# Query and key of the first head pair ahead, x's second half behind two weight tiles, one product for the gates' partial sums, and mLSTM heads that wait for their own value alone

## The chip, the cores and the metric

The kernel runs on one core of a Trainium2 chip. A core has a matrix engine (PE, with its weight loads shown as PEld), a vector engine (DVE), a scalar engine (ACT), GpSimd (POOL) and a sync engine (SP) that here only issues DMAs. They run side by side, each through its own queue in order, and wait for one another by semaphores. The metric is device time in microseconds (us) of one execution; lower is better.

## The reference

It is one inference step of a two-layer decoder trunk. It works on 512 prompt tokens and on 32 sample tokens (8 sequences of 4) that bring recurrent states along. Layer 0 has a combined mixer: one input projection feeds four mLSTM heads and four GLA heads, and one output projection joins them. Layer 1 has a Mamba-2 mixer. Each mixer and each squared-ReLU MLP is followed by a residual sum and a layer norm. Outputs are the tokens and all new states, in float32. What matters here is the first mixer:

```python
mq, mk, mv, mo, mi, mf, gq, gk, gv, gg, ga = split(x @ w_in)
ig, lf = mi + ig_bias, log_sigmoid(mf + fg_bias)          # mLSTM gates, per token and head
ml_out = headnorm(mlstm(mq, mk, mv, ig, lf)) * sigmoid(mo)
la = log_sigmoid(ga @ wa2 + ba) / 16                      # GLA decay, per token and key feature
gla_out = headnorm(gla(gq, gk, gv, la)) * silu(gg)
mix = concat(ml_out, gla_out) @ w_out
```

## The kernel before

Activations lie feature-major: 128 features on the partitions, 544 tokens (512 and 32) along the rows, in two halves of 272. A float32 product is made of three fp32r products, high by high, high by low and low by high, so weights and activations are each split into a high part (a cast on ACT) and the rest (a subtraction on DVE). One weight tile is 1024 by 128; `dense` (L365) works through one tile and one half with 24 matmuls (L378) that sum in PSUM, and an evacuation takes the sum out.

`WeightStream` loads tiles in planned order over SP into three raw buffers and splits them (L167, L168) ahead of use; five split tiles are held. `take_x` loads x in pieces of two feature blocks. In it the order on SP, ACT and DVE is the written one: tile 0 with x's first half piece by piece, tile 1, then tiles 2 to 4 (`ws.ahead(HEAD)`), then x's second half (L295 on SP) with its splits (L287, L288). Constants, the selector, `wa2` and small states are loaded behind it (`issue_after(x_in)`).

In `ab` the input projection has 24 tiles: gq, gq, gk, gk, four gv, two mq, two mk, four mv, four gg, four mo (two heads share a q or k tile, a v or gate tile is one head's). The first `HEAD` = 5 tiles run on the first half one after another and then on the second; the next run both halves each, and the last four run as a group again. `evac` copies a projection out; gate tiles (gg, mo) take five operations on ACT and one or two on DVE for each half, all others a plain copy.

PE's order is written out by hand. Everything that isn't projection sits in **lanes**, generators that yield a number of ticks. `tick` is called ahead of each projection matmul and lets every lane count down by one, or run on to its next yield. So small products are laced between projection products at places set by the table `W` and by `need(key)`, which polls once a tick. The lanes are:

- `gla_lane`: waits for the gates, makes the decays (`la`, L1032, then a chain over ACT and DVE to `A`), and then scores for two head pairs q: query times key of the diagonal (`gd`, L1068), then nine levels of a halving scheme, each with a POOL subtraction F (L1079), two exponentials on ACT, `zq` and `zk` on DVE, and products `gs` (L1096, L1109), `W["lev"]` ticks apart. Then come the four heads (`head_out`: `num` L865, a norm over DVE and ACT to `hn`, its transpose `hot` L899), the final state, and the samples of GLA and mLSTM.
- `ml_lane`: `ml_gates`, then one pipeline of four heads (`ml_head`: `rowbc` L769; exponentials E on ACT; the masked key `kz` L1310; `md` and `mo` L1314 to L1321; then `head_out`), `W["mr"]` ticks between steps. In a full step PE issues `hot` of one head, `md` and `mo` of the next but one, `num` of the one between, and `rowbc` of the last. It starts when GLA is ready, mq and mk are there, and `mvt` says that all four values are in token order.
- the value lane: `tokmajor` transposes each value W["v"] = 24 ticks after its tile.

The gate projection (4 + 4 + 16 columns) doesn't go through `dense`: `gate_sums` multiplies eight narrow weight blocks in four column groups at a time, so a half's partial sums lie in four groups of 32 partitions; `gate_rows` (L849) joins them with three products of 4, 4 and 16 columns, and three ACT operations (L851) add the bias. `until("mheads")` in the last group of tiles runs the mLSTM lane to its end if it hasn't got there.

Of the kernel before, what the change touches and what calls it, by code (L numbers as in the profile page):

```python
# [31 lines left out]
HEAD, TAIL = 5, 7  # L32
HEADM = 6

W = dict(dec=12, gates=30, gr=8, sc=16, lev=14, v=24, kd=10, out=38, ss=40, end=12, c0=20, u=13, s=16, ml=12, mr=40, dt=238, sg=72, sx=14, sq=26, so=48, l0=12, l1=12, v0=74, v1=55, f0=16, f1=18, f2=4, ls=20, vs=47)
GATES = ((0, 0, 4), (32, 4, 4), (64, 8, 16))
# [20 lines left out]
def _consts():  # L57
    c = {}
    i = np.arange(P)
    c["ident"] = np.eye(P)  # L60
    for L in LEVELS:
        s, t = i[:, None], i[None, :]
        m = (s // (2 * L) == t // (2 * L)) & (s % (2 * L) < L) & (t % (2 * L) >= L)
        c[f"lv{L}"] = m[:, i % (2 * L) >= L]
    c["hm"] = np.stack([i < 64, i >= 64], 1)
    hs = np.zeros((P, 2, P))
    for h in range(4):
        hs[h, h // 2, (h % 2) * 64:(h % 2) * 64 + 64] = 1
    c["hfeat"] = hs
    hq = np.zeros((P, P)); hq[i // 32, i] = 1  # L70
    c["hstk"] = hq
    i4 = np.zeros((P, 4)); i4[:4] = np.eye(4)
    c["i4"] = i4
    c["hmask"] = i[:, None] // 32 == np.arange(4)[None]
    s, t = (i % 32)[:, None], np.arange(32)[None]
    c["smask"] = (s // LS == t // LS) & (s <= t)
    c["seye"] = s == t
    c["sl2"] = (s // 4 == t // 4) & (s % 4 < 2) & (t % 4 >= 2)
    c["sl1"] = (s // 2 == t // 2) & (s % 2 < 1) & (t % 2 >= 1)
    c["seqm"] = (i % 32)[:, None] // LS == np.arange(NB)[None]  # L80
    r = np.ones(T); r[NP::LS] = 0
    c["rmask"] = np.broadcast_to(r, (P, T))
    sel = np.zeros((P, 4, P))
    for h in range(4):
        sel[h, h] = 1
        sel[32 + h, h] = 1
    off, cols = {}, []
    n = 0
    for k, v in c.items():
# [139 lines left out]
def trunk_kernel(ctx, tc, a, stages=("ab", "mlp0", "ssd", "mlp1")):  # L229
# [61 lines left out]
    def take_x(pool, bufs=12, first=None):  # L291
# [8 lines left out]
        with tc.high_priority(), tc.manual_schedule(engines=order):  # L300
            ts = [load(S, 0, k)[0] for k in range(0, KT, 2)]
            S.preload_act_table_set("natural_log_exp_and_others")

            def step(k):
                cut(0, 2 * k, ts[k])
                if k == 1 and first is not None:
                    first()
            ws._emit([lambda k=k: step(k) for k in range(KT // 2)])
            ws._emit([lambda: None] * 4)
            ws.ahead(HEAD)  # L310
            for k in range(0, KT, 2):
                t, loaded = load(nc.sync, 1, k)
                ts.append(t)
                cut(1, k, t)
        with tc.issue_after(loaded):
            nc.sync.dma_start(out=lnp, in_=a["lnp"])
# [399 lines left out]
    def ab(pool, early, then):  # L716
# [19 lines left out]
        S.copy(selr, selt)  # L736
        prm = pool.tile([P, 13], F32, name="prm", bufs=1)
        G.dma_start(out=prm, in_=a["ab_prm"])
# [36 lines left out]
        gate = ft("gate")  # L775
        G.memset(gate[64:96], 0.0)
        fm = {}
# [3 lines left out]
        def tokmajor(key, h):  # L781
# [8 lines left out]
            for b in range(4):  # L790
                TE.transpose(p[:, b * P:(b + 1) * P], x[:, b * P:(b + 1) * P], ident)
            S.copy(vt[key][:, :, h, :128], p.rearrange("p (b c) -> p b c", b=4))
            G.tensor_copy(vraw[key][:, h], x[:, NP:])
            if h == 3:
# [9 lines left out]
        def evac(m, hf, ps):  # L804
# [20 lines left out]
            if hf == 1:  # L825
                ready.add(key)

        order = [(k, i) for k, n in (("gq", 2), ("gk", 2), ("gv", 4), ("mq", 2), ("mk", 2),
                                                     ("mv", 4), ("gg", 4), ("mo", 4)) for i in range(n)]

# [13 lines left out]
        def gate_rows(hf):  # L844

            c0, c1 = HALVES[hf]
            p = pm("gates")
            for o, c, n in GATES:
                TE.matmul(p[o:o + n, :TH], C("seye")[:, c:c + n], gsum[hf], start=True, stop=True)  # L849
            for o, c, n in GATES:  # L850
                S.activation(gate[o:o + n, c0:c1], p[o:o + n, :TH], AF.Identity, bias=gbias[o:o + n])  # L851
            if hf == 1:
                ready.add(("gate", 0))

        def head_out(mx, key, h, sT, enm=None):


            pp = [pm("num"), pm("num")]
            w = 128 if enm is None else 130
# [164 lines left out]
        def gla_decay():  # L1024
            gla["A"] = []
            for q in range(2):
                A = ft("A")
                t = ft("lat")
                for hf in range(2):
                    c0, c1 = HALVES[hf]  # L1030
                    p = pm("la")
                    TE.matmul(p[:, :TH], wa2[64:96, q * P:(q + 1) * P], gate[64:96, c0:c1], start=True, stop=True)  # L1032
                    S.activation(t[:, c0:c1], p[:, :TH], AF.Abs, bias=ba[:, q:q + 1])
# [8 lines left out]
        def gla_scores():  # L1042
# [4 lines left out]
            gla["kst"] = []  # L1047
            A, Q, K = gla["A"], [fm["gq", i] for i in range(2)], [fm["gk", i] for i in range(2)]
            zk = []
            for j in range(2):  # L1050
# [6 lines left out]
            n = 0  # L1057
            for q in range(2):
                sT = gla["sT"][q] = early.tile([P, 10, 2, P], F32, tag="sT", name="sT", bufs=2)

# [85 lines left out]
        def gla_sample_scores():  # L1146
# [3 lines left out]
            for L, mk in ((0, "seye"), (1, "sl1"), (2, "sl2")):  # L1150
# [24 lines left out]
                if L:  # L1175
                    V.copy_predicated(sst, C(mk).bitcast(U32), p[:, :NS])
                else:
                    V.tensor_tensor(sst, p[:, :NS], C(mk), ALU.mult)
            ready.add("sscores")
# [187 lines left out]
        def gla_lane():  # L1367
# [3 lines left out]
            yield from gla_decay()  # L1371
            yield from need(("gq", 1), ("gk", 1))
            yield from gla_scores()
# [8 lines left out]
            yield from gla_samples()  # L1382
            yield from need("mscores")
            yield from ml_samples()

        def ml_lane():
            ml["cg"] = []
            yield from need(("gate", 0))
            yield from ml_gates()
            yield from need("gla", ("mq", 1), ("mk", 1), "mvt")  # L1390
            rows_bc(ml["nM"][:, :NP])
# [17 lines left out]
        lanes.setdefault("ss", [])  # L1409
        heads = [ws.next() for _ in range(HEAD)]  # L1410
        for hf in range(2):
            for _ in gate_sums(1) if hf else ():
                pass
            for m, w in enumerate(heads):
                if hf and 1 <= m <= 2:
                    gate_rows(m - 1)
                dense(w, xrhs, KT, hf, lambda h, p, m=m: evac(m, h, p), first=(hf, m) == (0, 0))
        for m, key in enumerate(order[:-4]):
            if m >= HEAD:
                w = ws.next()  # L1420
# [594 lines left out]
def layout(i):  # L2015
# [15 lines left out]
    o["ab_gate"] = _blocks(g, 32)[0]  # L2031
    o["ab_in"] = _blocks(np.concatenate([seg(n) for n in ("gq", "gk", "gv", "mq", "mk", "mv", "gg", "mo")], 1), P)
    o["ab_out"] = _blocks(i["ab_w_out"][0], P)
    prm = np.zeros((P, 13), w.dtype)
    prm[0:4, 0], prm[32:36, 0] = i["ab_ig_bias"][0], i["ab_fg_bias"][0]
# [78 lines left out]
```

## Time and profile before

| what | us |
|---|---|
| median of three runs | 1495.31 (1493.13 to 1497.03) |
| profiled execution | 1494.75 |
| its span, first to last instruction | 1493.0 |
| input projection with its lanes (24 tiles, 1152 products) | ends at 246.7 |

The rest of the span is the output projection, two MLPs and the Mamba-2 mixer. In views of the trace a row gives the start in us, the us that it took, the engine, the line of the kernel, the operation, what it wrote and read, shapes and count; in brackets stands how long the engine had been idle and what ended it. Ends of matmuls are modelled, and one that is still draining counts as busy, so a wait can be longer for PE than its bracket says; the distance from start to start shows it. A float32 product with a full-precision operand has two records.

### The profile page before, as it was taken

The page shows a single profiled execution, that of the slowest core. Times are in us where ns is not written, and L with a number is a line of the kernel's source. Part 1 is how long each engine was busy: PE and PEld are TensorE (multiplying, and loading weights), DVE is VectorE, ACT ScalarE, POOL GpSimd, SP SyncE. Part 2 cuts the span into 40 slices and gives each one's busy share as a digit, 9 for nine tenths or more (in the row PEclk, how much of TensorE's full clock was granted, in tenths as well). Part 3 has the DMA queues.
Part 4 walks back from the last instruction along what each step waited for, and adds up shares of the span by engine and source line. Part 5 has one row for each costly group of instructions (what it writes and reads, how often), then busy time and mean ns, then how long its engine had stood idle before and what let it go on. Part 6 is the DMA issues. An engine that isn't in the chain of part 4 may idle for free.

```text
span 1493.0 us, 29232 instructions
## 1 busy us (share of the span) xinstructions
PE 1468.9 (98%) x11615; PEld 1417.0 (95%) x11615; DVE 1096.6 (73%) x2075; ACT 795.1 (53%) x1754; POOL 191.5 (13%) x225
## 2 busy tenths in 40 slices
PE   9999999999999999999999999999999999999997
PEld 8899989999999999999888789899999999999996
DVE  4966577786676667678999978777588677676656
ACT  6645556483543544547786676555257354444333
POOL 1510222100000000010244341421010000000000
PEclk9999999999999999999999999999999999999998
DMA  7221315313333332525567766364222333233121
GB/s 239 84 73 44 103 58 167 90 55 99 96 102 92 93 91 80 156 72 183 131 176 232 248 183 217 100 214 143 72 75 71 96 100 99 86 100 98 58 86 60
DMA packets 95025, 172.51 MB, mean 116 GB/s; under 512 B 15896, under 2 KB 50968, under 8 KB 94632
## 3 DMA queue, kind: packets, MB, share of 16 engines
q1 hardware_dynamic: 62280, 140.46, 30.7%
q10 hardware_dynamic: 29216, 17.19, 4.5%
q0 software_dynamic: 3392, 12.99, 2.4%
q8 instruction: 91, 1.49, 0.4%
q14 instruction: 46, 0.38, 0.1%
HBM read 153.48 MB, written 17.13 MB: 114 GB/s over the span
## 4 chain that ended last, share of the span: by engine, by line
PE 42%; DVE 4%; DMA 2%; issue 1%; ACT 1%; POOL 0%; SPq 0%; DVEq 0%; POOLq 0%; ACTq 0%
PE psd L378 29%; PE psd L590 9%; DVE wlo L168 1%; PE yp L1694 1%; DMA ec<-d_ecs 1%; DVE acc L1588 1%; PE it L1741 1%; DMA E<-d_cs 1%; PE sp L1672 1%; DMA wraw<-mlp_w 0%; PE sps L1748 0%; DVE h0n L1754 0%; PE ip L1669 0%; ACT E L1654 0%; PE xt L1633 0%
## 5 line engine op out<-in xcount | busy, mean ns | idle before, releaser
L378 PE MATMUL psd<-xh,whi 128*128 128x272 f32 x1488 | 441.5, 297 | 0.0
L378 PE MATMUL psd<-xh,wlo 128*128 128x272 f32 x1488 | 435.3, 293 | 0.0
L378 PE MATMUL psd<-xl,whi 128*128 128x272 f32 x1488 | 432.8, 291 | 1.3 <-DVE xl L478 1.3
L378 PEld LDWEIGHTS psd<-xh,whi 128*128 128x128 f32 x1488 | 280.9, 189 | 9.2 <-issue 6.9
L378 PEld LDWEIGHTS psd<-xl,whi 128*128 128x128 f32 x1488 | 281.1, 189 | 7.5 <-issue 4.5
L378 PE MATMUL psd<-hh,whi 128*128 128x272 f32 x992 | 286.6, 289 | 0.0
L378 PE MATMUL psd<-hlo,whi 128*128 128x272 f32 x992 | 286.1, 288 | 0.0
L378 PE MATMUL psd<-hh,wlo 128*128 128x272 f32 x992 | 286.0, 288 | 0.0
L378 PEld LDWEIGHTS psd<-xh,wlo 128*128 128x128 f32 x1488 | 280.8, 189 | 4.2 <-issue 3.2
L168 DVE TENSOR_TENSOR wlo<-wraw,whi 128x1024 fp32r<-128x1024 f32 (+2 forms) x175 | 207.9, 1191 | 56.4 <-ACT whi L167 55.5
L167 ACT CAST whi<-wraw 128x1024 fp32r<-128x1024 f32 (+2 forms) x175 | 173.5, 996 | 127.8 <-PE psd L378 113.0
L378 PEld LDWEIGHTS psd<-hlo,whi 128*128 128x128 f32 x992 | 186.7, 188 | 0.2
L378 PEld LDWEIGHTS psd<-hh,whi 128*128 128x128 f32 x992 | 186.8, 188 | 0.2
L378 PEld LDWEIGHTS psd<-hh,wlo 128*128 128x128 f32 x992 | 186.7, 188 | 0.1
L428 DVE TENSOR_TENSOR xf<-xf,psd 128x272 f32<-128x272 f32 x208 | 88.4, 435 | 74.3 <-PE psd L378 73.8
L590 PE MATMUL psd<-xh,wlo 128*128 128x272 f32 x416 | 119.9, 288 | 0.0
L590 PE MATMUL psd<-xh,whi 128*128 128x272 f32 x416 | 119.8, 288 | 0.0
L590 PE MATMUL psd<-xl,whi 128*128 128x272 f32 x416 | 119.6, 288 | 0.0
L203 ACT CAST whi<-wsum 128x1024 fp32r<-128x1024 f32 x52 | 54.3, 1044 | 111.4 <-PE psd L590 70.1
L203 ACT CAST whi<-wraw 128x1024 fp32r<-128x1024 f32 (+1 forms) x52 | 43.4, 834 | 95.3 <-PE psd L378 84.2
L204 DVE TENSOR_TENSOR wlo<-wsum,whi 128x1024 fp32r<-128x1024 f32 x52 | 63.7, 1225 | 23.2 <-ACT whi L203 23.2
L590 PEld LDWEIGHTS psd<-xl,whi 128*128 128x128 f32 x416 | 78.4, 188 | 0.0
(487 smaller groups left out, 2832.3 us busy)
## 6 DMA issues: line engine op xcount, KB each, us to landing
wraw<-mlp_w SPq DMA_DIRECT2D x80, 512.0 KB, 3.6
wraw<-ssd_in SPq DMA_DIRECT2D x40, 512.0 KB, 4.1
wraw<-mlp_w SPq DMA_DIRECT2D x64, 256.0 KB, 3.1
wraw<-ab_in SPq DMA_DIRECT2D x22, 512.0 KB, 3.7
h<-h SPq DMA_DIRECT2D x32, 256.0 KB, 5.0
h0n<-h0n SPq DMA_DIRECT2D x16, 512.0 KB, 5.8
E<-d_cs ACTq DMA_DIRECT2D x16, 512.0 KB, 4.6
s_h<-h0n POOLq DMA_DIRECT2D x16, 512.0 KB, 4.1
```

Source lines behind the costliest of these rows:

```text
L167: nc.scalar.copy(hi[:, r], w[:, r])
L168: nc.vector.tensor_tensor(lo[:, r], w[:, r], hi[:, r].bitcast(F32), ALU.subtract)
L203: self.cut[0] = nc.scalar.copy(hi, x).ins
L204: self.cut[1] = nc.vector.tensor_tensor(lo, x, hi.bitcast(F32), ALU.subtract).ins
L378: last[0] = TE.matmul(ps[:, :TH], (hi, hi, lo)[t][:, k, :], (rh, rl, rh)[t], start=i == 0, stop=i == n - 1).ins
L428: V.tensor_tensor(x, x, ps, ALU.add)
L590: last[0] = TE.matmul(ps, wt[:, k], bt[:, k], start=first and n == 0, stop=n == 11, skip_group_check=not first).ins
L1588: V.scalar_tensor_tensor(acc[:, :n], ci[:, w:w + n], cw[:, m, w:w + 1], acc[:, :n], ALU.mult, ALU.add)
L1672: TE.matmul(sp, Bt[:, b], xw, start=True, stop=True)
L1694: TE.matmul(ypv[64 * e:64 * e + 64, j], z[:, 64 * r:64 * r + 64], E[:, r], start=True, stop=True)
L1741: TE.matmul(it[64 + NS * k:64 + NS * k + NS], Cm[:, NS * (q + k):NS * (q + k) + NS], h0[k], start=q == 0, stop=q == NB - 2)
```

## The change

Six edits, all in the first mixer. The order of the projection becomes gq0, gk0, gq1, gk1 (the weights are laid out so on the host), and only two tiles run on both halves one after another. x's second half is loaded and split behind weight tiles 0 and 1, ahead of tiles 2 to 4. The second half's gate sums follow its first tile, and both `gate_rows` follow the second tile. In `gate_rows` one product with a 128 by 128 selector `selg` replaces three, and one ACT operation over 128 partitions replaces three; the decay product takes all 128 rows. GLA scores of a head pair wait for that pair's query and key alone. The mLSTM lane no longer waits for `mvt`; the samples do, and `head_out` asserts that its own value is there. `lev` goes from 14 to 15 and `mr` from 40 to 46.

```diff
-W = dict(... lev=14, ... mr=40, ...)
+HEADA = 2
+W = dict(... lev=15, ... mr=46, ...)
...
-            ws.ahead(HEAD)
             for k in range(0, KT, 2):
                 t, loaded = load(nc.sync, 1, k)
                 ts.append(t)
                 cut(1, k, t)
+            ws.ahead(HEAD)
...
-        prm = pool.tile([P, 13], F32, name="prm", bufs=1)
+        prm = pool.tile([P, 13 + 32], F32, name="prm", bufs=1)
...
-        G.memset(gate[64:96], 0.0)
+        selg = pool.tile([P, P], F32, tag="sc", name="selg", bufs=4)
+        G.memset(selg, 0.0)
+        for o, c, n in GATES:
+            G.tensor_copy(selg[:, o:o + n], prm[:, 13 + c:13 + c + n])
...
             S.copy(vt[key][:, :, h, :128], p.rearrange("p (b c) -> p b c", b=4))
+            ready.add((key + "vt", h))
...
-        order = [(k, i) for k, n in (("gq", 2), ("gk", 2), ("gv", 4), ("mq", 2), ("mk", 2),
-                                                     ("mv", 4), ("gg", 4), ("mo", 4)) for i in range(n)]
+        order = [(k, i) for i in range(2) for k in ("gq", "gk")]
+        order += [(k, i) for k, n in (("gv", 4), ("mq", 2), ("mk", 2), ("mv", 4), ("gg", 4), ("mo", 4)) for i in range(n)]
...
             p = pm("gates")
-            for o, c, n in GATES:
-                TE.matmul(p[o:o + n, :TH], C("seye")[:, c:c + n], gsum[hf], start=True, stop=True)
-            for o, c, n in GATES:
-                S.activation(gate[o:o + n, c0:c1], p[o:o + n, :TH], AF.Identity, bias=gbias[o:o + n])
+            TE.matmul(p[:, :TH], selg, gsum[hf], start=True, stop=True)
+            S.activation(gate[:, c0:c1], p[:, :TH], AF.Identity, bias=gbias)
...
+            assert (key + "vt", h) in ready
...
-                    TE.matmul(p[:, :TH], wa2[64:96, q * P:(q + 1) * P], gate[64:96, c0:c1], start=True, stop=True)
+                    TE.matmul(p[:, :TH], wa2[:, q * P:(q + 1) * P], gate[:, c0:c1], start=True, stop=True)
...
             for q in range(2):
+                yield from need(("gq", q), ("gk", q))
+                Q, K = {q: fm["gq", q]}, {q: fm["gk", q]}
...
             yield from gla_decay()
-            yield from need(("gq", 1), ("gk", 1))
             yield from gla_scores()
...
             yield from gla_samples()
-            yield from need("mscores")
+            yield from need("mscores", "mvt")
             yield from ml_samples()
...
-            yield from need("gla", ("mq", 1), ("mk", 1), "mvt")
+            yield from need("gla", ("mq", 1), ("mk", 1))
...
-        heads = [ws.next() for _ in range(HEAD)]
+        heads = [ws.next() for _ in range(HEADA)]
         for hf in range(2):
-            for _ in gate_sums(1) if hf else ():
-                pass
             for m, w in enumerate(heads):
-                if hf and 1 <= m <= 2:
-                    gate_rows(m - 1)
                 dense(w, xrhs, KT, hf, lambda h, p, m=m: evac(m, h, p), first=(hf, m) == (0, 0))
+                if (hf, m) == (1, 0):
+                    for _ in gate_sums(1):
+                        pass
+        for hf in range(2):
+            gate_rows(hf)
         for m, key in enumerate(order[:-4]):
-            if m >= HEAD:
+            if m >= HEADA:
```

The selector's columns come with `prm` (32 more, a repeated 32 by 32 identity), which also takes the place of the constant `seye` in the sample scores.

More of the change, by code (lines that the diff above doesn't have):

```diff
@@ L33 @@
 HEADM = 6
-W = dict(dec=12, gates=30, gr=8, sc=16, lev=14, v=24, kd=10, out=38, ss=40, end=12, c0=20, u=13, s=16, ml=12, mr=40, dt=238, sg=72, sx=14, sq=26, so=48, l0=12, l1=12, v0=74, v1=55, f0=16, f1=18, f2=4, ls=20, vs=47)
+HEADA = 2
+W = dict(dec=12, gates=30, gr=8, sc=16, lev=15, v=24, kd=10, out=38, ss=40, end=12, c0=20, u=13, s=16, ml=12, mr=46, dt=238, sg=72, sx=14, sq=26, so=48, l0=12, l1=12, v0=74, v1=55, f0=16, f1=18, f2=4, ls=20, vs=47)
 GATES = ((0, 0, 4), (32, 4, 4), (64, 8, 16))
@@ L76, in _consts @@
     c["smask"] = (s // LS == t // LS) & (s <= t)
-    c["seye"] = s == t
     c["sl2"] = (s // 4 == t // 4) & (s % 4 < 2) & (t % 4 >= 2)
@@ L1047, in gla_scores @@
             gla["kst"] = []
-            A, Q, K = gla["A"], [fm["gq", i] for i in range(2)], [fm["gk", i] for i in range(2)]
-            zk = []
+            A, zk = gla["A"], []
             for j in range(2):
@@ L1177, in gla_sample_scores @@
                 else:
-                    V.tensor_tensor(sst, p[:, :NS], C(mk), ALU.mult)
+                    V.tensor_tensor(sst, p[:, :NS], prm[:, 13:], ALU.mult)
             ready.add("sscores")
@@ L2031, in layout @@
     o["ab_gate"] = _blocks(g, 32)[0]
-    o["ab_in"] = _blocks(np.concatenate([seg(n) for n in ("gq", "gk", "gv", "mq", "mk", "mv", "gg", "mo")], 1), P)
+    b = _blocks(np.concatenate([seg(n) for n in ("gq", "gk", "gv", "mq", "mk", "mv", "gg", "mo")], 1), P)
+    o["ab_in"] = b[[0, 2, 1, 3, *range(4, 24)]]
     o["ab_out"] = _blocks(i["ab_w_out"][0], P)
-    prm = np.zeros((P, 13), w.dtype)
+    prm = np.zeros((P, 13 + 32), w.dtype)
+    prm[:, 13:] = np.arange(P)[:, None] % 32 == np.arange(32)
     prm[0:4, 0], prm[32:36, 0] = i["ab_ig_bias"][0], i["ab_fg_bias"][0]
```

## The prediction

> **What bounds the kernel now.** First the page's busy table, then the waits of the matrix engine (PE) in the first 420 us: engine and line that waited, for what, us in total, times, longest.
>
> ```profile
> PE 1468.9 (98%) x11615; PEld 1417.0 (95%) x11615; DVE 1096.6 (73%) x2075; ACT 795.1 (53%) x1754; POOL 191.5 (13%) x225
> ```
>
> ```profile
> PE gs L1096 <- DVE zk L1088: 2.3, 2, 1.5
> PE hot L899 <- ACT hn L893: 1.7, 3, 0.7
> PE warm L1402 <- DVE ones L281: 1.1, 1, 1.1
> PE md L1314 <- ACT kz L1310: 0.8, 1, 0.8
> ```
>
> PE is the bound: 1493.0 − 1468.9 leaves 24.1 us idle in the whole span, and the change touches the first stage alone. So it can win little more than that stage's waits: `gs`, `hot` and `md`, and what hangs on them.
>
> Every lane step is placed by counting projection products (L378), so I asked the windows view for L378 alone. In the first bracket is their number up to each time.
>
> ```profile
> 0.00:14.40 14.40, 7.81 (x48) 6.92 (x49) 1.00 0.77 252
> 0.00:33.98 33.98, 25.40 (x181) 23.71 (x181) 1.00 0.73 247
> 0.00:108.70 108.70, 78.30 (x542) 70.68 (x542) 1.00 0.42 132
> 0.00:168.10 168.10, 119.29 (x818) 107.98 (x818) 0.99 0.33 105
> 0.00:195.20 195.20, 138.07 (x941) 124.41 (x941) 0.99 0.35 108
> ```
>
> The code gives the same counts. Gates are ready at product 168; one tick for the need, 12 for `dec` and one to advance: first `la` at 181. Scores start at 217, first `gs` at 249, first GLA head at 542, GLA ready at 737, `mvt` at 768 + 25 + 25 − 1 = 817, first mLSTM `rowbc` at 818, then a step every 41: the fourth at 941. The drain `until("mheads")` stands at 1056. So counting tells where PE meets a lane step. What a product costs shows in an undisturbed stretch: 33.00/263 = 0.1255 us.
>
> ```profile
> 239.00:272.00 33.00, 33.00 (x263) 33.00 (x264) 20.58 (x41) 14.88 (x32) 3.86 (x5) 1.00 0.51 138
> ```
>
> The dearest place is the fourth mLSTM step. Here is PE's timeline (start, us, what; in brackets idle time before), and below it the next, undisturbed step:
>
> ```profile
> 194.38 0.28 PE L378 MATMUL psd<-xl,whi 128*128 128x272 f32 x1
> 195.26 1.03 PE L899 MATMUL hot<-con,hn 128*128 128x128 f32 x3 [0.59 <-ACT hn L893]
> 196.63 0.33 PE L899 MATMUL hot<-con,hn 128*128 128x128 f32 x1 [0.34 <-ACT hn L893]
> 197.75 1.44 PE L1314 MATMUL md<-mq,kz 128*128 128x128 f32 x8 [0.80 <-ACT kz L1310]
> ...
> 203.87 0.48 PE L769 MATMUL rowbc<-rb,selr 128*128 128x256 f32 x2
> ```
>
> ```profile
> 212.07 0.60 PE L899 MATMUL hot<-con,hn 128*128 128x128 f32 x4
> ...
> 216.85 0.37 PE L378 MATMUL psd<-xl,whi 128*128 128x272 f32 x1
> ```
>
> From 194.38 to 203.87 are 9.49 us. One product (0.13) and the undisturbed step from `hot` to the end of `num` (216.85 − 212.07 = 4.78) explain 4.9: **4.6 us are lost.** The windows view splits them (busy us of PE, PEld, DVE, ACT, POOL; then the granted clock):
>
> ```profile
> 143.88:147.29 3.41, 3.41 (x27) 3.10 (x25) 0.75 (x1) 0.00 (x0) 0.62 (x1) 1.00 0.31 120
> 147.29:150.70 3.41, 3.41 (x16) 3.40 (x16) 0.88 (x5) 0.73 (x2) 0.00 (x0) 0.50 0.00 0
> 184.00:195.00 11.00, 10.67 (x85) 10.13 (x83) 8.16 (x37) 5.35 (x15) 1.39 (x2) 1.00 0.44 126
> 195.07:198.48 3.41, 2.04 (x10) 1.28 (x11) 1.63 (x4) 2.95 (x8) 1.34 (x2) 1.00 0.25 96
> 198.48:201.90 3.42, 3.42 (x12) 2.63 (x12) 1.72 (x5) 0.43 (x1) 1.56 (x3) 0.50 0.00 0
> ```
>
> After the window with the waits the clock is 0.50 for 3.42 us, which is 1.7 of the 4.6. A second drop follows at 147.29 without any wait, behind the tiny `sc` products: 16 products in 3.41 us, 3.41 − 16 × 0.1255 = 1.4 us lost.
>
> [...]
>
> **The change, part by part.**
>
> *Order.* By the new code two tiles come first, in both halves: gates at 96, `la` at 110 and 123, scores start at 136, first `gs` at 169 (then 16 apart with `lev` 15), heads from 480, GLA ready at 675. Values are in token order at 649, 697, 745 and 793; the mLSTM starts at 676, steps at 723, 770, 817, 864, 911 and 958 (47 apart), and ends at 1005, ahead of the drain at 1056. No `num` (770, 817, 864, 911) comes ahead of its value. `ml_samples`, which now waits for all values (817), is reached at 832: no wait. None of this adds or removes PE work; it moves it.
>
> *One product for three.*
>
> ```profile
> 27.81 0.65 PE L849 MATMUL gates<-gsum,con 128*4 128x272 f32 x6
> ```
>
> ```profile
> 272.42 0.62 PE L458 MATMUL mu<-lns,ones 128*128 128x272 f32 x2
> ```
>
> The three (six records, 0.65 us) already run side by side, and one full product of 272 columns takes 0.62: 0.03 a half, **−0.1** for both, rounded up. Counting records would have promised 2 × 0.43. [...] The `la` product with 128 rows for 32 streams the same 272 columns: 0. Building `selg` and its wait for `prm` stand on POOL, idle for 37.81 us before its first F (row below): 0. Three gate copies become one on ACT: two thirds of 1.48 us (row below) freed, per half.
>
> *x's second half.*
>
> ```profile
> 7.25 4.90 SPq L166 DMA_DIRECT2D wraw<-ab_in  x3
> 12.20 0.91 SPq L295 DMA_DIRECT2D xin<-xT  x2
> ```
>
> ```profile
> 18.91 0.45 SPq L742 DMA_DIRECT2D wa<-wa2p  x1
> ```
>
> ```profile
> xin<-xT SPq DMA_DIRECT2D x4, 272.0 KB, 5.4
> ```
>
> ```profile
> wa<-wa2p SPq DMA_DIRECT2D x1, 128.0 KB, 7.7
> ```
>
> ```profile
> 18.42 1.35 DVE L288 TENSOR_TENSOR xl<-xin,xh 128x544 fp32r<-128x544 f32 x2
> ```
>
> PE wants it after product 48, at 14.4 us, where it was 120. Its four issues on SP move from 12.20 to 7.25, past three weight tiles. With 5.4 us to landing the first piece is there at 12.7 and split at 14.0 (0.7 on ACT, 0.7 on DVE), the others about 0.7 apart, while PE takes 6 × 0.1255 = 0.75 over each. Behind the waiting splits stand, in written order on ACT and DVE, the casts of weight tiles 2 to 4; tile 2 is due after product 96, at 20.4 or later, so they have 4 us. `wa2`, issued behind x, landed at 18.91 + 7.7 = 26.6. Five us earlier it is there at 21.6; `la` at 110 comes at 20.4 + 2 × 0.62 + 14 × 0.1255 = 23.4 at the earliest. Taken: 0, at the edge; bounds 0 and +2 (both covers gone).
>
> *First GLA levels.*
>
> ```profile
> 33.12 1.48 ACT L851 ACTIVATE gate<-gates,prm 4x272 f32<-4x272 f32 x3
> 34.62 1.33 ACT L1063 ACTIVATE qm<-gq,con 128x512 f32<-128x512 f32 x2
> ...
> 37.19 0.87 ACT L1033 ACTIVATE lat<-la,prm 128x272 f32<-128x272 f32 x2
> ```
>
> ```profile
> 47.79 0.66 DVE L1088 TENSOR_TENSOR zk<-gk,F 128x256 f32<-128x256 f32 x1
> ```
>
> ```profile
> 43.38 1.86 POOL L1079 TENSOR_TENSOR F<-A 128x512 f32<-128x512 f32 x1 [37.81 <-DVE A L1038]
> ```
>
> From the first `la` at 33.99 to `zk` at 48.45 the chain over ACT, DVE, POOL, ACT and DVE took 14.5 us, and PE was there 1.5 us before it. The new order leaves 169 − 110 = 59 products where there were 249 − 181 = 68: 9 × 0.1255 = 1.1 us less. But 2.6 us of the old chain (34.62 to 37.19) are ACT doing `qm` and gate copies; `qm` now has its query before the gates. I let the 2.3 us become 1.8: **−0.5**. Bounds: 0 left (−2.3), and 1.1 more at each of the first two levels and nothing freed (+2.2).
>
> *GLA heads.*
>
> ```profile
> 124.80 1.38 PE L899 MATMUL hot<-con,hn 128*128 128x128 f32 x4 [0.73 <-ACT hn L893]
> ```
>
> `hot` waited 0.73 here and took 1.38 for the undisturbed 0.60: 1.5 us in all, its chain sharing DVE with `ml_gates`. That neighbour comes along unchanged (same `out`, same needs); only the projection's evacuations fall elsewhere. **−0.6**; bounds −1.5 and, if the second such wait grows to the size of the first, +1.
>
> *mLSTM steps.* The wait at 195 is for ACT: `hn` is late, `kz` behind it, then the clock falls. Each step now has 47 products for 41, 0.75 us more, and the first two lie beside value tiles, with one plain copy a half, instead of gate tiles. That covers part of the lateness. I take 1.2 us lost over all steps instead of 4.6: **−3.4**; bounds −4.6 and +9.2 (third rival).
>
> *Clock drop at `sc`.* The same products in the same neighbourhood; whether one window is filled by them depends on where the window falls: **−0.7**, half of 1.4; bounds −1.4 and 0.
>
> Sum: −0.1 − 0.5 − 0.6 − 3.4 − 0.7 = **−5.3 us**. The profiled execution took 1494.75 us (span 1493.0 and 1.75 around it), so 1489.45. It lies 0.6 under the median of the runs, 1495.31, within their range of 4 us. I predict 1489.5.
>
> **Rivals.** (1) *The lateness moves along*: another step pays the 4.6, now because samples and gate tiles meet there. For it: from 184.00 to 195.00 DVE was busy 8.16 of 11 us and ACT 5.35, yet `hn` was late; the order on them decides, not the load. Against: 0.75 us more in each step. Time: 1494.75 − 1.9 = 1492.9. (2) *All goes*: 0.1 + 2.3 + 1.5 + 1.4 + 4.6 = 9.9 us less, 1484.9. Against: the neighbours of `hot` and `sc` are the same. (3) *Slower*: the steps at 817, 864 and 911 lie beside state reads and updates of both samples as well as gate tiles. Once the chain from one step's `num` to `hn` is longer than 47 products and the step's 5.1 us of own PE work (11.0 us), each waits and drops the clock: 3 × 4.6 = 13.8 for 4.6, so 1494.75 + 9.2 − 0.3 = 1503.7. Against: the old step at 212.07 lay beside a sample and gate tiles too and lost nothing. (4) *It doesn't start earlier*, if something but `mvt` holds the mLSTM: GLA at 675 is the last of the others, so it does; I give this nothing.
>
> **The numbers.** About 0.3% (4.5 us) is what a measurement can tell here. Forecast 0.52 (its own range 1487 to 1492), rival 1 0.26, rival 2 0.10, rival 3 0.12. Faster means under 1490.8: four fifths of the forecast, 0.41, and rival 2, 0.51 together. Slower is rival 3, 0.12; the rest, 0.37, is no change. The range runs from rival 2, 1484.5, past rival 1 with late x and late levels (+2, +2.2), to 1497.5; it leaves out rival 3 and the tails.
>
> **What would show it.** L378 counts of 110 before the first `la`, 169 before the first `gs`, 676 before the first `rowbc`, 817 before the fourth step, and there no wait over 1 us and no window at clock 0.50; `gates` with two records near 0.6 us. I am wrong if PE waits for `xl` near 14 us or for `wa2` near 24, if `gs` waits over 3 us in all, or if a step after 676 is followed by clock 0.50.

## The result: slower by 0.3%, and the profile after

The changed kernel takes 1499.20 us (median of 12 runs, 1497.01 to 1502.62) where the kernel before, on the same chip, takes 1494.53 (12 runs, 1493.13 to 1497.03): ratio 1.003, 95% interval 1.0021 to 1.0039. I had predicted 1489.5 and a range up to 1497.5. The profiled execution took 1500.9 us, its span 1499.2, 6.2 longer than before's.

Busy table of the page, then the waits of PE in the first 420 us (us in total, times, longest):

```profile
PE 1470.2 (98%) x11607; PEld 1420.4 (95%) x11607; DVE 1094.2 (73%) x2075; ACT 795.2 (53%) x1750; POOL 190.1 (13%) x228
```

```profile
PE gs L1100 <- DVE zk L1092: 3.8, 1, 3.8
PE supd L1006 <- POOL vm L1002: 3.1, 1, 3.1
PE hot L902 <- ACT hn L896: 1.7, 2, 0.9
```

The work is the same, the waits are not. Where they arise shows when the start of each Nth projection or MLP product (written to `psd`: L378, and in later stages L395 and L590) is set against before's: the 1152nd, the end of the projection, comes 5.50 us late (252.16 for 246.66), and the difference stays at 5.50 up to product 2100; another 0.6 comes with a stretch at half clock at 735 us, in a stage that the change doesn't touch. So the explanation has to lie in the first 250 us.

The windows view of L378 alone, up to the first `la`, the first `gs`, the first `rowbc` and the fifth step's `hot` (number of products in the first bracket):

```profile
0.00:24.37 24.37, 15.71 (x109) 14.12 (x109) 1.00 0.87 301
0.00:40.08 40.08, 24.23 (x168) 21.81 (x168) 0.99 0.71 236
0.00:147.05 147.05, 100.03 (x674) 90.25 (x674) 0.97 0.34 108
0.00:193.45 193.45, 128.57 (x862) 115.14 (x862) 0.97 0.33 105
```

The places are within two products of those that counting gave (110, 169, 676, 864). What stands there isn't ready.

**The first level.** Timeline of ACT from the first `la` (24.37) on, then of DVE, POOL and PE (start, us; in brackets the idle time before and its releaser):

```profile
24.89 0.50 ACT L853 ACTIVATE gate<-gates,prm 128x272 f32<-128x272 f32 x1
25.27 1.05 ACT L167 CAST whi<-wraw 128x1024 fp32r<-128x1024 f32 x1
26.35 0.65 ACT L1219 COPY rw<-gate 4x544 f32<-4x544 f32 x1
27.02 0.65 ACT L1220 COPY uw<-gate 4x544 f32<-4x544 f32 x1
27.58 0.84 ACT L1036 ACTIVATE lat<-la,prm 128x272 f32<-128x272 f32 x2
...
34.60 0.44 ACT L1086 ACTIVATE F<-F 128x256 f32<-128x256 f32 x1
```

```profile
31.32 1.29 DVE L1041 TENSOR_TENSOR_SCAN A<-con,lat 128x544 f32<-128x544 f32 x1
...
33.21 2.00 DVE L168 TENSOR_TENSOR wlo<-wraw,whi 128x1024 fp32r<-128x1024 f32 x1
35.13 2.12 DVE L1041 TENSOR_TENSOR_SCAN A<-con,lat 128x544 f32<-128x544 f32 x1
37.18 1.26 DVE L1074 TENSOR_TENSOR sT<-gd,con 128x512 f32<-128x512 f32 x2
38.36 1.33 DVE L1090 TENSOR_TENSOR zq<-F,qm 128x512 f32<-128x512 f32 x1
39.61 0.41 DVE L1092 TENSOR_TENSOR zk<-gk,F 128x256 f32<-128x256 f32 x1
```

```profile
32.70 6.44 POOL L1083 TENSOR_TENSOR F<-A 128x512 f32<-128x512 f32 x4 [25.58 <-DVE A L1041]
```

```profile
40.08 2.08 PE L1100 MATMUL gs<-zq,zk 128*128 128x128 f32 x8 [3.83 <-DVE zk L1092]
```

Read it backwards. The exponentials of F end at 35.04, but `zq` starts at 38.36, 3.32 us later: the rest of a weight tile, the scan of the *second* head pair and the masks of `gd` stand ahead of it on DVE. Further up, ACT takes `la` 3.21 us after PE began it, behind a gate operation, a cast and two copies. Before, it was 3.20 us (33.99 to 37.19): other work stands where the change took work away. From `la` to the end of `zk` are 15.65 us (before: 14.46), and PE arrives with 59 products instead of 67. In before the last exponential of the first F and `zq` lay 0.29 us apart, and the scan of the second pair stood *behind* that `zk` (which started at 47.79):

```profile
45.62 0.43 ACT L1082 ACTIVATE F<-F 128x256 f32<-128x256 f32 x1
```

```profile
46.34 0.93 DVE L1086 TENSOR_TENSOR zq<-F,qm 128x512 f32<-128x512 f32 x1
...
48.37 2.18 DVE L1038 TENSOR_TENSOR_SCAN A<-con,lat 128x544 f32<-128x544 f32 x1
```

From start to start the wait is 3.99 us. Windows around it (PE, PEld, DVE, ACT, POOL busy; granted clock):

```profile
35.81:39.22 3.41, 0.44 (x4) 0.22 (x2) 3.41 (x4) 1.79 (x6) 3.33 (x3) 0.98 0.58 154
39.22:42.63 3.41, 2.55 (x11) 2.55 (x12) 3.06 (x5) 1.40 (x4) 2.03 (x2) 0.50 0.00 0
42.63:46.04 3.41, 3.41 (x17) 3.41 (x17) 1.74 (x3) 1.18 (x4) 1.47 (x2) 0.52 0.00 0
```

The half clock lasts until about 45.9: from 40.08 that is 5.8 us, so 2.9 lost by halving, an estimate, and 6.9 in all. From product to product it is 6.7: from the 168th to the 200th, with two groups of `gs` between, are 12.53 us, over the next such stretch 5.80. Before, with its two waits of 1.63 and 1.00, the like stretch (248th to 278th) took 8.82 us and the next 5.62: 3.2 lost. The first levels cost 3.5 us more.

**The steps.** The step at product 862 waits, as the fourth did before, and the clock falls again; then an update product of the mLSTM samples waits for POOL:

```profile
192.65:196.06 3.41, 2.27 (x12) 1.51 (x13) 1.84 (x5) 2.72 (x8) 0.65 (x2) 1.00 0.03 13
196.07:199.48 3.41, 3.41 (x12) 2.62 (x11) 1.79 (x3) 0.00 (x0) 0.73 (x1) 0.50 0.00 0
```

```profile
192.28 0.29 PE L378 MATMUL psd<-xh,whi 128*128 128x272 f32 x1
193.45 1.38 PE L902 MATMUL hot<-con,hn 128*128 128x128 f32 x4 [0.88 <-ACT hn L896]
195.10 1.23 PE L1318 MATMUL md<-mq,kz 128*128 128x128 f32 x8 [0.28 <-ACT kz L1314]
...
201.22 0.37 PE L378 MATMUL psd<-xl,whi 128*128 128x272 f32 x1
```

From product to product are 8.94 us; undisturbed, the same step takes 4.91 (0.13 and 4.78, as in the prediction). So 4.0 are lost, where before's fourth step lost 4.6. Here is POOL ahead of the update product:

```profile
206.09 1.63 POOL L1002 TENSOR_TENSOR vm<-vstk,con 128x390 f32<-128x390 f32 x2
211.21 0.76 POOL L916 TENSOR_TENSOR cg<-cg,gg 128x272 f32<-128x272 f32 x1 [3.49 <-DVE gg L826]
211.91 2.20 POOL L325 DMA_DIRECT2D xf<-xT  x4
216.95 0.69 POOL L916 TENSOR_TENSOR cg<-cg,gg 128x240 f32<-128x240 f32 x1 [2.84 <-DVE hf L892]
217.61 2.78 POOL L1002 TENSOR_TENSOR vm<-vstk,con 128x260 f32<-128x260 f32 x4
```

The third `vm` needs 0.6 us, but stands behind a gate product `cg` whose `gg` leaves DVE only at 216.87: POOL idles 2.84 us ahead of it (the bracket names a DVE operation that ended at the same moment). PE waits 3.3 us from start to start.

### The profile page after: what moved, and what is told of

It is laid out like the page before. It is cut to its first block, busy times and chain, and to the rows that moved or that the text cites. A ratio compares the mean times of both kernels' runs of the same rounds, so it can differ in the third digit from the quotient of the medians.

```text
span 1499.2 us, 29203 instructions
## 1 busy us (share of the span) xinstructions
PE 1470.2 (98%) x11607; PEld 1420.4 (95%) x11607; DVE 1094.2 (73%) x2075; ACT 795.2 (53%) x1750; POOL 190.1 (13%) x228
## 4 chain that ended last, share of the span: by engine, by line
PE 42%; DVE 4%; DMA 3%; ACT 1%; issue 1%; POOL 0%; SPq 0%; ACTq 0%; DVEq 0%; POOLq 0%
PE psd L378 29%; PE psd L590 9%; DMA E<-d_cs 1%; PE yp L1698 1%; PE it L1745 1%; DVE acc L1592 1%; DVE wlo L168 1%; DMA ec<-d_ecs 1%; PE sp L1676 1%; PE sps L1752 1%; DMA wraw<-mlp_w 0%; DVE h0n L1758 0%; ACT E L1658 0%; PE xt L1637 0%; PE ip L1673 0%
## 5 line engine op out<-in xcount | busy, mean ns | idle before, releaser
L378 PE MATMUL psd<-xh,whi 128*128 128x272 f32 x1488 | 441.6, 297 | 0.5 <-ACT xh L287 0.5
L378 PE MATMUL psd<-xh,wlo 128*128 128x272 f32 x1488 | 435.9, 293 | 0.0
L378 PE MATMUL psd<-xl,whi 128*128 128x272 f32 x1488 | 434.3, 292 | 1.3 <-DVE xl L478 1.3
L378 PEld LDWEIGHTS psd<-xh,whi 128*128 128x128 f32 x1488 | 281.6, 189 | 8.8 <-issue 6.1
L378 PEld LDWEIGHTS psd<-xl,whi 128*128 128x128 f32 x1488 | 281.8, 190 | 7.4 <-issue 4.3
L378 PE MATMUL psd<-hh,whi 128*128 128x272 f32 x992 | 286.6, 289 | 0.0
L378 PE MATMUL psd<-hh,wlo 128*128 128x272 f32 x992 | 286.2, 288 | 0.0
L378 PE MATMUL psd<-hlo,whi 128*128 128x272 f32 x992 | 286.1, 288 | 0.0
L378 PEld LDWEIGHTS psd<-xh,wlo 128*128 128x128 f32 x1488 | 281.5, 189 | 3.9 <-issue 2.9
L378 PEld LDWEIGHTS psd<-hlo,whi 128*128 128x128 f32 x992 | 186.7, 188 | 0.2
L378 PEld LDWEIGHTS psd<-hh,whi 128*128 128x128 f32 x992 | 186.8, 188 | 0.2
L378 PEld LDWEIGHTS psd<-hh,wlo 128*128 128x128 f32 x992 | 186.7, 188 | 0.1
L590 PE MATMUL psd<-xh,wlo 128*128 128x272 f32 x416 | 119.9, 288 | 0.0
L590 PE MATMUL psd<-xh,whi 128*128 128x272 f32 x416 | 119.8, 288 | 0.0
L590 PE MATMUL psd<-xl,whi 128*128 128x272 f32 x416 | 119.6, 288 | 0.0
L590 PEld LDWEIGHTS psd<-xl,whi 128*128 128x128 f32 x416 | 78.4, 188 | 0.0
```

Source lines behind the costliest of these rows:

```text
L378: last[0] = TE.matmul(ps[:, :TH], (hi, hi, lo)[t][:, k, :], (rh, rl, rh)[t], start=i == 0, stop=i == n - 1).ins
L590: last[0] = TE.matmul(ps, wt[:, k], bt[:, k], start=first and n == 0, stop=n == 11, skip_group_check=not first).ins
```

## The experiments

Theory A: the losses are separate waits, made by the early order (first level, then the samples' update and an mLSTM step that meet other neighbours), each of which can be taken away by itself. Theory B: the mLSTM part costs the time. Theory C, set up after the first four runs: PE arrives early at whatever is next late, so a wait taken away is paid at the next place. Each run stands against before on its own chip (1495.00, 1494.14 and 1495.26 us for the three groups of four). "Wait" columns are PE's extra distance from start to start over the usual one; "half clock" counts the stretches of about 3.4 us at 0.50 up to 250 us; the last column sets products 1152 and 10000 (of 10104) against before's 246.66 and 1466.47 us. These columns are of the one profiled execution, which can lie 1.9 to 2.6 us above its run's median (e5, e6, e8) or below it by as much (e12).

| run | median us | ratio [95%] | first `gs` wait | `supd` wait | `hot` wait of a step | half clock | at 1152 / 10000 |
|---|---|---|---|---|---|---|---|
| before |  |  | 1.63 (+1.00) |  | 0.75 | 2 | 0 |
| the change | 1499.20 | 1.0030 [1.0021, 1.0039] | 3.99 | 3.30 | 1.04 | 4 | +5.50 / +6.17 |
| e1_one_product | 1491.95 | 0.9976 [0.9967, 0.9986] | 1.44 (+1.01) |  | 0.75 | 1 | -3.28 / -1.66 |
| e2_order_alone | 1495.01 | 1.0004 [0.9992, 1.0017] | 3.99 |  |  | 1 | -1.51 / -0.08 |
| e3_ml_alone | 1491.16 | 0.9975 [0.9964, 0.9987] | 1.62 (+1.01) |  | 1.31 | 0 | -4.62 / -4.90 |
| e4_scores_later | 1491.58 | 0.9975 [0.9966, 0.9985] | 0 (third: 2.05) | 1.81 | 1.67 | 1 | -3.11 / -3.24 |
| e5_vm_first | 1499.24 | 1.0038 [1.0024, 1.0052] | 3.97 | 3.29 | 1.17 | 4 | +5.12 / +7.14 |
| e6_ml_later | 1494.95 | 1.0008 [0.9998, 1.0018] | 4.00 |  |  | 3 | +0.28 / +2.67 |
| e7_product_and_ml | 1487.43 | 0.9955 [0.9940, 0.9970] | 1.43 (+1.01) |  | 0.84 | 0 | -7.21 / -7.84 |
| e8_decay_split | 1497.80 | 1.0025 [1.0015, 1.0035] | 2.77 | 3.30 | 0.81 | 2 | +0.86 / +4.93 |
| e9_vm_early | 1496.59 | 1.0014 [1.0001, 1.0027] | 3.98 | 1.35 | 1.12 | 3 | +1.82 / +3.39 |
| e10_slack16 | 1492.96 | 0.9983 [0.9974, 0.9993] | 1.47 | 1.63 + 0.74 |  | 1 | -3.39 / -3.15 |
| e11_e7_slack20 | 1488.74 | 0.9961 [0.9946, 0.9976] | 0 (second: 1.32) | 0.48 | 1.57 | 0 | -7.51 / -6.27 |
| e12_gd_later | 1496.47 | 1.0015 [1.0005, 1.0025] | 1.72 | 3.30 | 0.54 | 1 | -0.45 / -0.89 |

**Parts alone.** e1: before with the single gate product and `selg`; the rest as before.

```diff
-            for o, c, n in GATES:
-                TE.matmul(p[o:o + n, :TH], C("seye")[:, c:c + n], gsum[hf], start=True, stop=True)
-            for o, c, n in GATES:
-                S.activation(gate[o:o + n, c0:c1], p[o:o + n, :TH], AF.Identity, bias=gbias[o:o + n])
+            TE.matmul(p[:, :TH], selg, gsum[hf], start=True, stop=True)
+            S.activation(gate[:, c0:c1], p[:, :TH], AF.Identity, bias=gbias)
...
-                    TE.matmul(p[:, :TH], wa2[64:96, q * P:(q + 1) * P], gate[64:96, c0:c1], start=True, stop=True)
+                    TE.matmul(p[:, :TH], wa2[:, q * P:(q + 1) * P], gate[:, c0:c1], start=True, stop=True)
...
```

> The kernel before, with the one product over 128 columns, its one ACT operation and the 128-row decay product alone. Theory A (the loss of the changed kernel is the first GLA level, whose chain now stands behind casts of freed weight tiles, and one wait of an update product for POOL): no effect beyond 1 us either way, 1494.5. Theory B (the mLSTM part costs the time, by a step wait that moves on and by the update that waits for POOL): the same. Both are wrong if it differs by over 2 us.

It gained 3.0 us; neither theory had that. PE's timeline of before (a decay product and the projection product behind it), then of e1 (gates, decay):

```profile
37.12 1.18 PE L1032 MATMUL la<-gate,wa 32*128 32x272 f32 x4
38.23 0.40 PE L378 MATMUL psd<-xh,wlo 128*128 128x272 f32 x1
```

```profile
28.03 0.62 PE L850 MATMUL gates<-gsum,selg 128*128 128x272 f32 x2
28.29 0.49 PE L377 MATMUL psd<-xh,whi 128*128 128x272 f32 x1
...
36.10 1.08 PE L1032 MATMUL la<-gate,wa 128*128 128x272 f32 x4
36.81 0.49 PE L377 MATMUL psd<-xh,wlo 128*128 128x272 f32 x1
```

Busy time hardly differs (0.65 and 0.62 for the gates), the distance to the next product does: 0.26 instead of 28.39 - 27.81 = 0.58, and 0.71 instead of 1.11 for `la`, which now takes all 128 rows (the second pair; the first took 1.31). Over both halves and both pairs that is 0.6 and 1.0; the first `gs` wait is 0.19 shorter. Most of the rest of the 3.28 is the stretch at half clock behind `sc`, absent from this profile. ACT does come to `lat` sooner here, 2.18 us behind `la` for 3.20, and the chain to the end of `zk` shrinks from 14.46 to 13.39 us; the wait hardly shrinks, because PE has 0.9 us less to do ahead of it as well.

e2: the change with the old mLSTM part; e3: before with the new one.

```diff
-mr=46
+mr=40
...
-            yield from need("mscores", "mvt")
+            yield from need("mscores")
...
-            yield from need("gla", ("mq", 1), ("mk", 1))
+            yield from need("gla", ("mq", 1), ("mk", 1), "mvt")
```

(for e3 the same lines the other way round, in before.)

> The changed kernel with the old mLSTM part (it waits for all four values again, mr 40). Theory A: the first gs still waits 3 to 4 us for zk with the clock at 0.50 near 40 us, no update product waits for POOL, the fourth mLSTM step waits as before; 3 to 4 us over the kernel before, 1498. Theory B: near the kernel before, 1494.5.

> The kernel before with the new mLSTM part alone (starts at GLA, mr 46, samples wait for the values). Theory A: first levels as before (2.3 us of waits), a step wait of 0 to 4.6 us somewhere, and the update waits for POOL only if the early heads bring it; between 1491 and 1497, likeliest 1494. Theory B: 3 to 5 us over the kernel before, 1498.5.

B falls by e3: the mLSTM part alone gains 3.8 us, where B had 3 to 5 lost. By e2 it wouldn't: B had 1494.5 there, A 1498, and 1495.01 was measured, no change, although e2 holds the gate product that gives 3.0. A was right that e2 keeps the whole first wait and has no wait for POOL. It was wrong on the mLSTM step at product 941: that one waits 0.77 us and keeps the clock, so the new order by itself already takes away much of what e3 takes away. In e3 the step at 925 loses 1.6 us instead of 4.6; another 1.5 of its 4.62 is the absent stretch behind `sc`.

e7: before with the gate product and the mLSTM part, without the new order.

> The kernel before with the single gate product and the new mLSTM part, the old order of tiles and of x. Each alone gave 3.0 and 3.8 us. Theory A (they save separate waits): 1488 us, ratio 0.9955; at product 1152 some 6 to 8 us ahead of before. Theory C (they draw on the same few microseconds of waits and of half clock): 1491 to 1492, ratio 0.9975.

It reached 1487.43, faster than both kernels, and the two gains add up. From it to the change is 11.8 us by medians, 12.7 at product 1152: that is what the new order of tiles costs beside the other two parts. Beside the gate product alone it costs 3.1 (e2 against e1), so most of it comes of the order and the early mLSTM together. Waits of PE in e7:

```profile
PE gs L1096 <- DVE zk L1088: 2.1, 2, 1.3
PE hot L899 <- ACT hn L893: 1.4, 2, 0.7
```

**The first level.** e4: 32 products between the decays and the scores.

```diff
             yield from gla_decay()
+            yield 31
             yield from gla_scores()
```

> The changed kernel with the scores of the first head pair 32 products later, so that 91 products instead of 59 lie between the first decay product and the first gs; all later GLA and mLSTM steps move by 32. Theory A: the first gs waits under 0.5 us, no clock drop near 40 us; 6 us under the changed kernel as far as later waits stay, 1493.5. Theory B: the gs wait goes as well but later steps keep or grow their waits, 1497 or more.

The first `gs` no longer waits; the third does, and heads and mLSTM come later as well, so e4 alone doesn't say which of the two gained. e6 delays only the mLSTM lane by the same 32 (a `yield 31` ahead of its `rows_bc`), e10 both, the scores by 16 and the mLSTM by 32.

> The changed kernel; the mLSTM lane alone starts 32 products later (its steps near 755, 802, 849, 896 products), GLA scores where the change puts them. Theory A: the first GLA levels keep their wait near 40 us (3.8 us and the half clock after it), so what the delayed scores won (7.6 us, with both lanes later) is split: the wait of the update product and of the mLSTM step shrink together by 3 to 6 us, 1493.5 to 1496, ratio 0.999 to 1.001. Rival (all that the delayed scores won was won at the first GLA levels): within 1 us of the changed kernel, 1498.5 to 1500, ratio 1.003. Theory C: as the rival.

> The changed kernel; GLA scores 16 products later, the mLSTM lane 32 products later, as in the run in which it alone was late (1494.95 us, first gs wait 4.0 us): the two differ in these 16 products ahead of the first level alone. Theory A (a chain of fixed length on DVE, ACT and POOL against a count of products): 16 products are 2.0 us, so the first gs waits 1.9 to 2.1 us instead of 4.0 and the time falls by 2 us, by 3.7 if the half clock behind it goes too: 1491 to 1493, ratio 0.998 to 0.999. Rival (the chain shares queues with the casts and comes later when the scores come later): the wait stays above 3 us and the time within 1 us of 1495.

e6 keeps the first wait of 4.0 us and gains 4.25 by the medians: `supd` and the step no longer wait (a samples' output `sho` does, 2.14), and one stretch at half clock follows the first `gs` instead of two. e10 against e6 moves the first levels, and with them GLA's heads and samples, by 16 products; the mLSTM steps stay. The wait falls from 4.00 to 1.47, by 2.5 us for 2.0 us of slack, as the masks of `gd` now come behind `zq` on DVE (the chain takes 14.43 us, in e6 15.38). The time falls by 2.0, or by 3.7 with each set against before on its own chip (ratios 0.9983 and 1.0008), as at product 1152.

```profile
PE mkt L1364 <- ACT hn L896: 2.1, 1, 2.1
PE supd L1006 <- POOL E L1310: 1.5, 1, 1.5
PE gs L1100 <- DVE zk L1092: 1.3, 1, 1.3
```

(waits of PE in e10.) e8 and e12 shorten the chain instead: e8 puts the second pair's decay 60 products later, in a lane of its own; e12 also issues `gd` and its masks behind the first level's `zq` and `zk`.

```diff
-            yield from gla_decay()
+            gla["A"] = []
+            yield from gla_decay(0)
+            yield W["dec"]
+            launch(later(60, gla_decay(1)), "dec")
             yield from gla_scores()
...
```

> The changed kernel; only the decay of the second head pair (one la product pair, its four operations on ACT and DVE and its scan of 2.1 us) is put 60 products later, out of the way of the first pair's chain; scores start where they did. Theory A (the chain of the first level stands behind other work on ACT and DVE): the wait of the first gs falls from 3.9 us to under 2, by the 2.1 us of the scan and the copies ahead of it, and the half clock after it goes or shrinks by half: 4 to 6 us less, 1493.5 to 1495.5, ratio 0.999 to 1.0005. Rival (the chain itself is too long for 59 products whatever lies beside it): the wait stays above 3 us and the time within 1.5 us of the changed kernel.

DVE in e8:

```profile
31.75 2.06 DVE L168 TENSOR_TENSOR wlo<-wraw,whi 128x1024 fp32r<-128x1024 f32 x1
33.73 1.27 DVE L1074 TENSOR_TENSOR sT<-gd,con 128x512 f32<-128x512 f32 x2
34.93 1.32 DVE L1090 TENSOR_TENSOR zq<-F,qm 128x512 f32<-128x512 f32 x1
36.18 1.31 DVE L1092 TENSOR_TENSOR zk<-gk,F 128x256 f32<-128x256 f32 x1
```

Without the second pair's decay the chain from `la` to the end of `zk` is 2.4 us shorter (13.24 for 15.65). The wait falls by 1.2 alone, because PE comes 1.2 us sooner too: it has no second pair of `la` products on its way, and waits less for the gate. `wlo` and the masks still stand ahead of `zq`, so the wait is neither under 2 us, as A had it, nor above 3. At product 1152 the run is 4.64 us ahead of the change, A's 4 to 6; the median is only 1.4 below. The profile shows a loss behind the projection, in the Mamba mixer that no kernel here changes: between products 5000 and 5500 this execution falls back by 3.9 us. PE's waits there, 757 to 775 us, in e8 and then in before:

```profile
PE yp L1706 <- DVE ec L1682: 2.8, 1, 2.8
```

```profile
PE yp L1694 <- DVE ec L1670: 0.8, 1, 0.8
```

DVE does a `wlo` of 2.10 us ahead of `ec`, and half clock follows at 769. A stretch at half clock between 720 and 851 us stands in eight of the thirteen changed kernels' profiles, so it isn't e8's own. Whether an earlier or later projection brings it about or a single execution shows it by chance is open.

e12 holds e8's edit and this one:

```diff
...
+                    for e in range(2) if L == 1 else ():
+                        p = pm("gd")
...
+                        V.tensor_tensor(sT[:, 0:4, e], p.rearrange("p (b c) -> p b c", b=4),
+                                        ident[:, None, :].broadcast_to([P, 4, P]), ALU.mult)
...
```

> The changed kernel with the second pair's decay put later (1497.8 us, first gs wait 2.8 us), and besides that the two diagonal products gd of a pair with their masks on DVE (1.3 us) put behind the first level's zq and zk. Theory A (DVE's queue decides when the first zk is there): the wait of the first gs falls to 1.3 to 1.8 us, 1495.5 to 1497 us, ratio 1.001 to 1.002. Rival (the wait is POOL's F and the exponentials behind it): it stays at 2.5 to 2.8 us, ratio 1.0025.

With the masks gone too the wait is 1.72 (a later level waits 0.92), and the time is A's. So DVE's queue is what lengthens the chain: it takes 12.62 us in e12, less than before's 14.46. In e12 `zq` (34.33) starts 0.2 us behind the exponentials (34.13), as it did before, and little of that queue is left in the wait of 1.72. What ACT's casts and copies ahead of `lat`, or the `wlo` of 33.21, cost by themselves wasn't tried.

**The update product.** e5 gives `vm` a higher priority for the planner; e9 writes the three `vm` of a head pair to POOL's queue together.

```diff
+                vms = []
                 for b0, b1 in ((0, 3), (3, 6), (6, 8)):
...
-                    yield W["u"]
+                    vms.append(vm)
+                for (b0, b1), vm in zip(((0, 3), (3, 6), (6, 8)), vms):
+                    nb = b1 - b0
+                    yield W["u"]
```

> The changed kernel; only the masked value vm of the samples goes ahead of waiting work on POOL. Theory A (the losses of the changed kernel are separate waits, each of which can be taken away by itself): the wait of the third mLSTM update product, 3.1 to 3.3 us at 218, is under 1 us and nothing else changes; 1496 us, ratio to before 1.001. Theory C (the matrix engine arrives early at whatever is next late, so a wait taken away is paid at the next place): the time stays within 1 us of the changed kernel, 1499, ratio 1.003, and a later wait of the first mixer grows by 2 to 3 us.

> The changed kernel; the three masked values vm of a head pair are written to POOL's queue together, ahead of the first update product, instead of one ahead of each (the attempt to move them by priority left POOL's order as it was, so it told nothing). Theory A: the third update product no longer waits 3.3 us at 218 (under 1 us), 1496 us, ratio to before 1.001. Theory C (paid at the next place): within 1 us of the changed kernel, 1499, ratio 1.003, and a later wait is 2 to 3 us longer.

e5 left POOL's order as it was, so its 1499.24 tells nothing of either theory. In e9 POOL does three `vm` ahead of the `cg` that waits; the wait goes from 3.30 to 1.35 (it is now the second pair's) and the time from 1499.2 to 1496.6, near A's 1496. In the profile part of the gain is something else: one stretch at half clock follows the first `gs` instead of two. POOL in e9:

```profile
204.34 2.21 POOL L1003 TENSOR_TENSOR vm<-vstk,con 128x390 f32<-128x390 f32 x3
209.50 0.76 POOL L916 TENSOR_TENSOR cg<-cg,gg 128x272 f32<-128x272 f32 x1 [2.95 <-DVE gg L826]
```

**Can e7 be bettered?** e11 gives e7 20 more products ahead of the scores (`yield 19`).

> The kernel before with the single gate product and the new mLSTM part (1487.4 us), and GLA scores 20 products (2.5 us) later, for the 2.4 us that its first two levels still wait. Theory A: these waits go and nothing takes their place, 1485 us, ratio 0.994. Theory C (a later start of GLA moves heads and mLSTM steps, which meet other work): 1487 to 1490, ratio 0.9955 to 0.997, with a new wait of 1 to 3 us in a level, a head or a step.

No: the two `gs` waits shrink from 2.44 to 1.32, but a step's `hot`, moved with them, waits 1.57 instead of 0.84, and a `supd` 0.48. Against before on its own chip it is 6.5 us faster, e7 6.7. Here theory C holds. In e4, e6 and e10 it holds in part: new waits of 1.6 to 2.2 us stand against a larger gain.

## Why the prediction was wrong, point by point

Two steps failed, the first GLA levels and the mLSTM steps, and both for one reason: I moved chains earlier without asking what else would then stand in the queues of DVE, ACT and POOL. Two of the signs of being wrong that I had named came: the first `gs` waits 3.99 us, and clock 0.50 follows the step at 862.

- **Order and places** were right: all counts came out within two products.
- **One product, -0.1:** sign right, size wrong. I compared busy lengths (0.65 and 0.62) where the distance to the next product decides; and I put `la` at 0 because it streams the same 272 columns, where the product over 128 rows instead of 32 saves 0.40 and more a pair (0.71 us to the next product in e1, 1.11 in before). About -1.6 from rows, -3.0 by e1's median.
- **x's second half, 0:** right; PE waited 0.5 us once, and product 72 is 0.1 us late.
- **First GLA levels, -0.5, bounds -2.3 and +2.2: the first step that failed.** It cost +3.5 (6.7 us lost instead of 3.2), outside the bounds. I had counted part of the 2.6 us that ACT did ahead of `lat` as freed. It wasn't: from `la` to `lat` are 3.21 us for 3.20, as a gate operation, a cast and copies fill the place. And I took the rest of the chain as fixed and didn't ask in which order DVE would take what else was ready by then. With the second pair's decay early, its scan got ahead of `zq`; a late `wlo` and the masks too, 3.32 us for 0.29. e8, e12 and e10 take the wait down step by step, 4.0 to 2.8 to 1.7, and to 1.5 by slack. I had also left out the clock here, though the prediction had shown it fall behind a wait.
- **GLA heads, -0.6:** no gain; `hot` waits 1.03 for 0.90.
- **mLSTM steps, -3.4, bounds -4.6 and +9.2: the second step that failed, and the larger miss.** In the old order mechanism and size held (e3: the step loses 1.6 us instead of 4.6). In the new order rival 1 came, a step that waits 1.04 + 0.50, has the clock at 0.50 for 3.41 us from 196.06 on and loses 4.0 of the 4.6; and on top a wait in none of my cases, `supd` for POOL, 3.3: together +2.7. I had checked that `ml_samples` finds its values at 832, but not what stands on POOL's queue where it then issues. That the bounds hold it is luck: they were set by rival 3.
- **Clock at `sc`, -0.7:** it fell again (141 us): 0. Over all profiles it is there in six and missing in eight, with the same products; that it turns on where a window falls was my estimate.
- **Range:** by its own terms rival 2 gives 1484.9 and the upper end 1497.1, where I wrote 1484.5 and 1497.5; it changes nothing.

Sum by the trace: -1.6 + 3.5 + 0.6 (second `la`, which waits for its gate) + 0.1 + (4.0 + 3.3 - 4.6) = +5.3, measured +5.50 at product 1152. Rival 3, my only way to slower, did not happen: one step waits, not three. What stays open is how much of a single execution is the position of the stretches at half clock: seven of the twelve variants lose 1.2 to 4.1 us behind product 1152, and each of the seven has such a stretch, e5 two, between 720 and 851 us, in stages that no kernel here changes.

## What to carry to other kernels

Moving a chain earlier moves it among other neighbours: list for each engine of the chain, in queue order, what else is ready by then, before subtracting anything from its length. Cost small products from start to start, next product included, not by busy length (here 0.26 us for 0.58, where the busy lengths were 0.62 and 0.65). Try the parts of a change alone and in pairs: here two of three gave 7 us, and the third took 12 back beside both, 3 beside one.

## What the runs showed of the hardware

- Up to 900 us half clock came in stretches of 3.41 us (6.83 is two), in each of the two profiles multiples of 3.413 us apart: 39.05, 141.45, 196.06 and 735.37 in the change, 147.28 and 198.48 in before. In the windows of 3.41 us ahead PE was busy 0.61 us (35.64 in the change), 2.27 (192.65, above) and, in before, 2.04 (195.07) and all 3.41 (143.88). In the change two windows with PE busy 2.01 and 1.68 us, at 213.13 and 216.54 around the wait of `supd`, had clock 1.00 behind them. So the busy time of the window ahead didn't decide it alone, and no row here shows what does. The same 4 us wait at the first `gs` was followed by 6.83 us at half clock, two such stretches, in the change and e5, and by one, 3.41 us, in e2, e6 and e9.
- Some DVE operations that began while an F ran on POOL were longer: `wlo` 2.00 us (33.21 in the change) and 2.06 (31.75 in e8) for 1.23, the scan 2.12 (35.13) for 1.29, `zq` 1.33 (38.36) for 0.68 (39.95 us in the change). The masks `sT`, which read a matmul's sum, were not (1.26 for two, where in before two without an F took 0.69 each, at 79.99 and 80.88). One that began ahead of an F kept its time, and the F was longer: `zq` at 39.95 took 0.68, the F of 40.17 behind it 1.39, where one alone took 1.05 (44.51). No row here shows what makes them longer.
